# A hybrid encoder layer on one core: weight blocks of `up_sums` loaded half an item later, pools changed ahead of the output additions, `h2d` loaded by ScalarE in pairs

## The chip, the cores and the metric

The kernel runs on one core of a Trainium2 chip. The metric is the device time of one execution in microseconds; less is better. The kernel before takes 2178.68 us, the median of three runs (2177.78 to 2183.35).

Names used below: PE is TensorE (PEld its weight loads), DVE is VectorE, ACT is ScalarE, POOL is GpSimd, SP is SyncE, whose queue issues most of the DMAs in order. "L863" is line 863 of the kernel before.

## What is computed

The reference is one layer of a streaming encoder for a prompt of 2048 tokens and a sample of 64, model width 1024, with states carried for the sample:

```python
h = rmsnorm(x, g1) * (1 + sc1) + sh1
proj = h @ w_in                          # pool input u, q, k, v, o, gates
pool_out = pool_mixer(u, ...)            # causal means of 2, 4, 8, 16 tokens
hs = mlstm_seq(q, k, v, gates, ...)      # 4 heads, chunks, state C, n, m
mix = concat([pool_out, norm(hs) * sigmoid(o)], -1) @ w_out
x = x + gt1 * mix
h2 = rmsnorm(x, g2) * (1 + sc2) + sh2
up = h2 @ w_up                           # width 2 * 2816
conv = b_conv + sum(w_conv[j] * upp[:, j:j + T] for j in range(3))
a, g = split(conv, 2, -1)
x = x + gt2 * ((silu(g) * a) @ w_down)
```

A final rmsnorm follows, and the new states are returned. Everything is in float32.

## The kernel before, in words

Every matrix product is done in three passes of float32r: a tile is split into a high part (a copy, by ACT) and a low part (a subtraction, by DVE), and high x high, high x low and low x high are added up in PSUM. Weights come from HBM as a stream in the order of use: `issue` (L384) loads the next unit, `work_on` (L407) splits it (L411 on ACT, L414 on DVE), and `pump` (L421) keeps several units ahead, at most five of them still unsplit.

**Attention half.** The tokens go in four groups (`for o in groups`, L1432): 512 tokens each, the last one with the 64 of the sample besides. A group runs `proj_v` (the v columns and the gates), then four heads with three products each (q, k, o: 12 calls of `gemm`), then the four pooling blocks, then `outproj` (L617): eight output rows of 128, the first two as a pair, then six single ones. In the last group the pair ends with `leave` (L1419), which works off the generators that are left, stores the states, closes the pools of the attention half (`actx`) and opens pool `f1`, whose tiles `fscr` and `ssum` take that memory.

**FFN half.** It works on three groups of 704 tokens. The up-projection uses a scheme of Strassen's kind: a 2 x 2 block product is done with seven products instead of eight, on sums of blocks. Sums of weight blocks come from `up_sums` (L844), those of the activations from `sums_of` (L757). For the first group `norm_sums` (L795) reads the normed rows from `h2d` in HBM into four `fscr` tiles, in pairs for each of four blocks `kc`, and writes seven named tiles of sums, high and low, into `hx`. For each name ACT writes the high part (L782) and DVE the low part (L768); DVE also forms the next sums in place (L764). The first FFN products (L1573) read `hx`: the first of them, B11, needs that name of all four blocks.

**What sets the order.** Side work is written as generators in five lists (`bg`). `tick(i)` (L106) takes one step of the first generator of list i, and `gemm` (L467) calls ticks at fixed places among its eight column blocks. `up_sums` is in list 4: `gemm` steps it after the blocks in `ups`, by default (1, 3, 4, 6), unless `quiet` is set, as it is from the pooling blocks until the pair of output rows is nearly done. `proj_v` steps it four times a group. `norm_sums` is in list 1, stepped seven times in an output row once `f1` is open. The steps only write the program down: within the attention half a planner then orders each engine's instructions by priority, which follows the order of writing, and by readiness in its own model of time. `keep_in_program_order` (here also `pin`) holds an instruction behind the one written before it on its engine. In the FFN half PE, ACT, DVE and POOL keep the order of writing. Semaphores are placed by the compiler. An engine's queue is in order: what waits at its head holds up all behind it. That is also true of DMA issues on SP and ACT.

**`up_sums`.** It starts in group 1, has 44 items (22 blocks f in two halves) and a ring of four tiles `w4`. Three items are loaded ahead (two DMAs each, L849). An item takes four steps: two empty ones, two DVE instructions (L863, L864), two more (L866, L867); then the item three ahead is loaded (L871) and this one is stored to `wsum` (L872). That load takes the tile whose store was issued an item earlier and has to wait for it.

Of the kernel before, what the change touches and what calls it, by code (L numbers as in the profile page):

```python
# [25 lines left out]
FT = 704  # L26
# [38 lines left out]
def tile_layer(ctx: ExitStack, tc: tile.TileContext, xT, vecs, cst, rst, w_mod, w_ada, w_qkou, w_v, w_pool,  # L65
               w_out, w_up, w_down, w_quad, st_C, st_pool, yT, o_pool, o_C, o_m, o_conv):
    nc = tc.nc
# [399 lines left out]
    def gemm(ps, W, mv, o, ks=None, order=None, late=None, ups=(1, 3, 4, 6)):  # L467
        order = order or list(range(len(mv)))
        ks = ks or order
        for k in ks:  # L470
            if late is not None and k == late:
                drain(0, 2)
            at = order.index(k)
            U = W.at(at // 4)
            for pi, (a, b) in enumerate(PASSES):
                for bi, (lo, hi) in enumerate(o.blks):
                    pe.matmul(ps[bi][:, :hi - lo], U[:, a, k % 4 * P:(k % 4 + 1) * P], mv[k][:, b, lo:hi],  # L477
                              start=(at == 0 and pi == 0), stop=(k == order[-1] and pi == 2))
            if at in (1, 2, 4, 6, 7):
                tick(0)  # L480
            if at in ups and not quiet:
                tick(4)
            if at == 3 and o.last and not spare:
                tick(1)
            if at == 4 and not quiet and not spare:
                tick(3)
            if spare and at in (1, 2, 3, 4, 5, 6):
                tick(1)
        for i in (1, 3):
            tick(i)  # L490
        for gen in list(bg[2]):
            if next(gen, 0) == 0:
                bg[2].remove(gen)
# [98 lines left out]
    def load_x(k, o):  # L592
        x = scr()
        nc.sync.dma_start(out=x[:, :o.T], in_=xT[k, :, o.t0:o.t0 + o.T])
        return x
# [18 lines left out]
        rstd_cols([ssum], o, out)  # L614
        yield

    def outproj(o, mix, between):  # L617

        order = [4, 5, 6, 7, 3, 2, 1, 0]
        ssum = None if o.last else ssum_tile()  # L620
        now = Urgent(nc.vector)
        nx = [load_x(n, o) for n in (0, 1)]
        for rows in [(0, 1)] + [(n,) for n in range(2, KD)]:
            xs = nx
            Ws = [Row() for _ in rows]
            pss = [[mm_ps() for _ in o.blks] for _ in rows]
            if len(rows) == 1:
                gemm(pss[0], Ws[0], mix, o, order=order, ups=(4,))
            else:
                for W, ps in zip(Ws, pss):  # L630
                    gemm(ps, W, mix, o, ks=order[:6], order=order)
                quiet.clear()
                for W, ps in zip(Ws, pss):
                    gemm(ps, W, mix, o, ks=order[6:], order=order, late=1)
            nx = [load_x(rows[-1] + 1, o)] if rows[-1] + 1 < KD else []
            for n, x, ps in zip(rows, xs, pss):
                for (bi, pa, pb, a, b, s) in o.pieces:
                    now.scalar_tensor_tensor(out=x[:, a:b], in0=ps[bi][:, pa:pb], scalar=gt1(n, s), in1=x[:, a:b],
                                             op0=ALU.mult, op1=ALU.add)
                nc.sync.dma_start(out=x2d[n, :, o.t0:o.t0 + o.T], in_=x[:, :o.T])  # L640
            if rows[0] == 0:
                between()
                if o.last:
                    ssum = fscr("ssum")
            for n, x in zip(rows, xs):
                sq_acc(ssum, x[:, :o.T], o.T, n == 0)
        if o.last:
            bg[0].append(stat2(o, ssum))
        else:
            side.append(rstd_rows(ssum, o, RS2[:, 4 * o.g:4 * o.g + len(o.chunks)], []))  # L650
# [12 lines left out]
    def fscr(dt=F32):  # L663
        if dt in ("rb", "ssum"):
            return spare[0].tile([P, FT], F32, tag=dt, name=dt)
        return spare[0].tile([P, FT], dt, tag="fscr", name="fscr", bufs=4)
# [128 lines left out]
    def norm_sums(o, B, scr):  # L795

        xs = {}

        def load(kc):
            xs[kc] = [scr(), scr()]  # L800
            for x, k in zip(xs[kc], (kc, kc + 4)):
                (act if kc < 2 else nc.sync).dma_start(out=x[:, :FT], in_=h2d[k])
        load(0)
        yield
        for kc in range(4):
            if kc < 3:
                load(kc + 1)
            yield from sums_of(xs.pop(kc), lambda nm: (B.at(nm, kc, 0), B.at(nm, kc, 1), lambda: None))

    def prepare(o, scr):  # L810

# [25 lines left out]
    if True:  # L837
# [6 lines left out]
        def up_sums():  # L844

            def load(f, c):
                w = a1.tile([P, 4, 256], F32, tag="w4", name="w4", bufs=4)
                for i in range(2):
                    tc.keep_in_program_order(nc.sync.dma_start(out=w[:, 2 * i:2 * i + 2, :], in_=w_up[NF * i + f].rearrange(  # L849
                        "p (h c) -> p h c", h=2)[:, :, c:c + 256]))  # L850
                return w
            todo = [(f, c) for f in range(NF) for c in (0, 256)]
            pin = tc.keep_in_program_order
            nx = [load(*todo[i]) for i in range(3)]
            yield
            yield
            for i, (f, c) in enumerate(todo):
                w = nx.pop(0)
                yield
                yield  # L860

                a0, a1_, g0, g1 = (w[:, i, :] for i in range(4))
                pin(dve.tensor_tensor(out=g1, in0=g0, in1=g1, op=ALU.add))  # L863
                pin(dve.tensor_tensor(out=g0, in0=a0, in1=g0, op=ALU.subtract))  # L864
                yield
                pin(dve.tensor_tensor(out=a0, in0=g1, in1=a0, op=ALU.subtract))  # L866
                pin(dve.tensor_tensor(out=a1_, in0=a1_, in1=a0, op=ALU.subtract))  # L867
                yield

                if i + 3 < len(todo):  # L870
                    nx.append(load(*todo[i + 3]))  # L871
                pin(nc.sync.dma_start(out=wsum[f, :, :, c:c + 256], in_=w))  # L872

        def fold():
# [541 lines left out]
        def nothing():  # L1416
            pass

        def leave():  # L1419

            drain(1, 2, 3, 4)
            nc.sync.dma_start(out=o_pool, in_=PO)
            nc.sync.dma_start(out=o_C[:, 0], in_=SP[0])
            nc.sync.dma_start(out=o_C[:, 1], in_=SN)
            nc.sync.dma_start(out=o_m[0], in_=M[:, GT:GT + 1])
            nc.sync.dma_start(out=o_m[1], in_=M[:, TMAX + 1:TMAX + 2])
            actx.close()
            spare.append(fctx.enter_context(tc.tile_pool(name="f1", bufs=1)))
            B.append(Sums())
            bg[1].append(norm_sums(fgroups[0], B[0], fscr))  # L1430

        for o in groups:  # L1432
# [61 lines left out]
                bg[2].append(pg)  # L1494
            drain(1)
            if o.last:
                outproj(o, mix, leave)
            else:
                bg[1].append(norm_apply(groups[o.g + 1], box, hn))
                outproj(o, mix, nothing)  # L1500
# [792 lines left out]
```

## Time and profile before

| what | value |
|---|---|
| median of the runs | 2178.68 us |
| profiled execution, its own time | 2178.68 us |
| its span, first to last instruction | 2176.9 us |
| granted TensorE clock, mean | 0.998 |
| DMA moved | 539.51 MB, mean 248 GB/s |
| PE on the chain that ended last | 83% of the span |
| DVE / DMA / issue on that chain | 7% / 6% / 2% |
| attention half | 0 to about 793 us |
| FFN half | from about 793 us |

How to read it: the profile is of one execution. A view of groups gives busy time, the mean duration of one instruction, and the idle time of the engine just before, with what ended it ("<-"). A view of waits gives who waited for whom: total us, times, longest. A busy PE isn't PE at its peak, since matmuls are pipelined. The view of stages gives the busy time of each engine in a stretch. The `x` counts instructions. "SPq" and "ACTq" are the DMA issues and waits of those queues.

### The profile page before, as it was taken

The numbers are of one execution on the slowest core, as the hardware profiler recorded it, in microseconds if no ns is written. First come the engines' busy times: TensorE is split into PE (matmuls) and PEld (weight loads), VectorE is DVE, ScalarE is ACT, GpSimd is POOL, SyncE is SP. The second block draws the span as 40 slices with busy tenths as digits, with TensorE's granted clock in tenths as the row PEclk, the third lists the DMA queues.
The fourth block names the chain that finished last, engine by engine and source line by source line (L and its number), as shares of the span: only waits on it lengthen the run. The fifth ranks groups of instructions, "written<-read, shape, count | busy, mean of one in ns | idle before, by whom it ended". The sixth has DMA issues, their size and how long they took to land.

```text
span 2176.9 us, 38052 instructions
## 1 busy us (share of the span) xinstructions
PE 2151.8 (99%) x13553; PEld 2044.1 (94%) x13553; DVE 1634.7 (75%) x3040; ACT 1094.2 (50%) x2181; POOL 252.3 (12%) x475
## 2 busy tenths in 40 slices
PE   8999999999999999999999999999999999999998
PEld 7888888888899999999999999999999999999998
DVE  5868669767855678797967669888887597887874
ACT  4554335234333456464736446655655364565554
POOL 0010000001000101010101120100100321111112
PEclk9999999999999999999999999999999999999999
DMA  8887997998879477798967976666668675555542
GB/s 323 326 300 229 311 310 261 312 293 277 299 242 310 133 268 257 265 314 286 347 220 253 313 251 222 238 201 218 229 211 272 231 257 182 172 177 189 174 160 81
DMA packets 297351, 539.51 MB, mean 248 GB/s; under 512 B 25760, under 2 KB 114336, under 8 KB 297160
## 3 DMA queue, kind: packets, MB, share of 16 engines
q1 hardware_dynamic: 287144, 513.31, 70.7%
q10 hardware_dynamic: 10016, 23.76, 2.8%
q8 instruction: 107, 1.75, 0.3%
q14 instruction: 84, 0.69, 0.1%
HBM read 410.98 MB, written 125.98 MB: 247 GB/s over the span
## 4 chain that ended last, share of the span: by engine, by line
PE 83%; DVE 7%; DMA 6%; issue 2%; ACT 2%; SPq 0%; POOL 0%; ACTq 0%; DVEq 0%; POOLq 0%
PE mm L1573 33%; PE mm L477 21%; PE mm L2139 12%; PE mm L2016 8%; PE mm L1118 2%; DVE wt L414 2%; DMA wt<-wsum 1%; DMA raw<-w_ada 1%; PE m L1308 1%; PE m L1330 1%; PE m L1328 1%; PE m L1293 1%; DMA w<-w_ada 1%; DVE tg L1551 1%; DMA raw<-w_qkou 0%
## 5 line engine op out<-in xcount | busy, mean ns | idle before, releaser
L1573 PE MATMUL mm<-hx,wt 128*128 128x352 f32 x5544 | 886.7, 321 | 3.3 <-DVE hx L768 2.4
L1573 PEld LDWEIGHTS mm<-hx,wt 128*128 128x128 f32 x5544 | 878.3, 188 | 6.3 <-DVE hx L768 3.2
L477 PE MATMUL mm<-hl,wt 128*128 128x512 f32 (+2 forms) x1920 | 387.4, 357 | 0.1
L411 ACT ACTIVATE wt<-raw 128x512 fp32r<-128x512 f32 (+3 forms) x470 | 276.7, 597 | 185.1 <-PE mm L477 63.9
L414 DVE TENSOR_TENSOR wt<-raw,wt 128x512 fp32r<-128x512 f32 (+3 forms) x470 | 313.5, 673 | 65.4 <-ACT wt L411 65.2
L477 PEld LDWEIGHTS mm<-hl,wt 128*128 128x128 f32 x1920 | 316.7, 189 | 47.7 <-issue 4.4
L2139 PE MATMUL mm<-av,wt 128*128 128x448 f32 (+1 forms) x1632 | 262.8, 322 | 0.0
L2139 PEld LDWEIGHTS mm<-av,wt 128*128 128x128 f32 x1632 | 250.5, 188 | 11.1
L1988 DVE SCALAR_TENSOR_TENSOR x<-mm,MOD,x 128x352 f32<-128x352 f32 (+3 forms) x360 | 168.0, 508 | 78.7 <-PE mm L2139 65.1
L2016 PE MATMUL mm<-av,wt 128*128 128x352 f32 x1344 | 220.6, 323 | 1.7 <-DVE x L1988 0.7
L2016 PEld LDWEIGHTS mm<-av,wt 128*128 128x128 f32 x1344 | 215.4, 188 | 4.8 <-DVE ea L1582 2.7
L1620 ACT ACTIVATE mm<-mm 128x352 f32<-128x352 f32 x196 | 87.8, 448 | 237.7 <-PE mm L1573 181.5
L477 PE MATMUL mm<-mx,wt 128*128 128x512 f32 (+1 forms) x960 | 182.6, 352 | 0.0
L477 PEld LDWEIGHTS mm<-mx,wt 128*128 128x128 f32 x960 | 159.3, 188 | 22.5
L1551 DVE SCALAR_TENSOR_TENSOR ta<-ea,V,ta 128x704 f32<-128x704 f32 (+1 forms) x132 | 125.7, 953 | 58.6 <-ACT ta L1546 54.6
L1551 DVE SCALAR_TENSOR_TENSOR tg<-eg,V,tg 128x704 f32<-128x704 f32 (+1 forms) x132 | 125.7, 952 | 56.6 <-ACT tg L1546 54.1
L414 DVE TENSOR_TENSOR wt<-wt 128x512 fp32r<-128x512 f32 x196 | 133.4, 687 | 8.6 <-ACT wt L411 8.6
L411 ACT ACTIVATE wt<-wt 128x512 fp32r<-128x512 f32 x196 | 119.2, 622 | 29.5 <-DMA wt<-wsum 28.5
L1529 POOL COPY ea<-UC 128x2 f32<-128x2 f32 x66 | 32.5, 493 | 505.5 <-DVE ta L1551 410.9
L1760 ACT ACTIVATE tg<-tg 128x704 f32<-128x704 f32 (+1 forms) x66 | 52.4, 795 | 71.6 <-DVE tg L1551 71.6
L1118 PE MATMUL mm<-wt,hl 128*128 128x256 f32 (+1 forms) x576 | 71.4, 284 | 0.0
L1118 PEld LDWEIGHTS mm<-wt,hl 128*128 128x128 f32 x576 | 70.4, 190 | 0.8 <-issue 0.6
(305 smaller groups left out, 2202.1 us busy)
## 6 DMA issues: line engine op xcount, KB each, us to landing
wt<-wsplit SPq DMA_DIRECT2D x132, 512.0 KB, 4.3
raw<-w_up SPq DMA_DIRECT2D x198, 256.0 KB, 4.0
wt<-hl_kept SPq DMA_DIRECT2D x96, 512.0 KB, 6.1
wt<-wsum SPq DMA_DIRECT2D x132, 256.0 KB, 5.2
wsplit<-wt SPq DMA_DIRECT2D x66, 512.0 KB, 5.5
w<-w_up SPq DMA_DIRECT2D x88, 256.0 KB, 3.7
wsum<-w SPq DMA_DIRECT2D x44, 512.0 KB, 4.9
Bd<-fscr ACTq DMA_DIRECT2D x56, 352.0 KB, 4.1
```

Of the source, the lines that this page charges most:

```text
L411: act.activation(u.w[:, 0, :u.n], u.raw[:, :u.n], AF.Copy)
L414: dve.tensor_tensor(out=u.w[:, 1, :u.n], in0=u.raw[:, :u.n], in1=u.w[:, 0, :u.n].bitcast(F32), op=ALU.subtract)
L477: pe.matmul(ps[bi][:, :hi - lo], U[:, a, k % 4 * P:(k % 4 + 1) * P], mv[k][:, b, lo:hi], start=(at == 0 and pi == 0), stop=(k == order[-1] ...
L1118: pe.matmul(ps[ti][:n, :cols], h[4 * kh + k4][:, b, lo:lo + n], U[:, a, k4 % 2 * cols:(k4 % 2 + 1) * cols], start=(kh == 0 and k4 == 0 and ...
L1529: pool.tensor_copy(ext[:, 0:2], UC[:, f, :])
L1551: dve.scalar_tensor_tensor(out=t[:, :E], in0=ext[:, j:j + E], scalar=wc(j, f), in1=t[:, :E], op0=ALU.mult, op1=ALU.add)
L1573: pe.matmul(bk.t[:, :FH], U[:, a, kc * P:(kc + 1) * P], Bo.at(nm, kc, b), start=(first and kc == 0 and pi == 0), stop=(kc == 3 and pi == 2 ...
L1620: act.activation(to.t[:, :FH], bk.t[:, :FH], AF.Copy)
L1760: act.activation(self.tg[:, :E], self.tg[:, :E], AF.Silu)
L1988: dve.scalar_tensor_tensor(out=x3[n][:, a:b], in0=bk.t[:, a - lo:b - lo], scalar=gt2(n, s), in1=x3[n][:, a:b], op0=ALU.mult, op1=ALU.add)
L2016: pe.matmul(bk.t[:, :FH], U[:, a, c:c + P], quad.put(op, m, b), start=(first and m == 0 and pi == 0), stop=(m == 1 and pi == 2), skip_grou ...
L2139: pe.matmul(bks[i].t[:, :hi - lo], U[:, a, k % 4 * P:(k % 4 + 1) * P], av[k][:, b, lo:hi], start=(k == 0 and (a, b) == PASSES[0]), stop=(k ...
```

## The change

It has four parts.

1. `outproj` steps `up_sums` after blocks 2 and 5 of a single row, where it was after block 4 alone.
2. In `outproj` `between` (in the last group: `leave`) is called ahead of the additions to the output rows, where it was behind them. The stores of the states are taken out of `leave` into `states`, which is called behind the first of the pair's two last gemm parts, when the heads are done.
3. `norm_sums` issues all loads of `h2d` on ACT. Two blocks are loaded at the first step, the third and fourth behind the second name of the block before. Before, one block was loaded ahead and the next one at the beginning of each block, the last two on SP.
4. `up_sums` loads an item in the first of the two empty steps, two items ahead, behind the store of the item before. The number of loaded items at the start is the same.

```diff
-    def outproj(o, mix, between):
+    def outproj(o, mix, between, behind_heads=None):
...
-                gemm(pss[0], Ws[0], mix, o, order=order, ups=(4,))
+                gemm(pss[0], Ws[0], mix, o, order=order, ups=(2, 5))
...
                 for W, ps in zip(Ws, pss):
                     gemm(ps, W, mix, o, ks=order[6:], order=order, late=1)
+                    if behind_heads:
+                        behind_heads()
+                        behind_heads = None
             nx = [load_x(rows[-1] + 1, o)] if rows[-1] + 1 < KD else []
+            if rows[0] == 0:
+                between()
             for n, x, ps in zip(rows, xs, pss):
...
-            if rows[0] == 0:
-                between()
-                if o.last:
-                    ssum = fscr("ssum")
+            if rows[0] == 0 and o.last:
+                ssum = fscr("ssum")
...
-                (act if kc < 2 else nc.sync).dma_start(out=x[:, :FT], in_=h2d[k])
-        load(0)
+                act.dma_start(out=x[:, :FT], in_=h2d[k])
+        for kc in (0, 1):
+            load(kc)
         yield
         for kc in range(4):
-            if kc < 3:
-                load(kc + 1)
-            yield from sums_of(xs.pop(kc), lambda nm: (B.at(nm, kc, 0), B.at(nm, kc, 1), lambda: None))
+            for i, _ in enumerate(sums_of(xs.pop(kc), lambda nm: (B.at(nm, kc, 0), B.at(nm, kc, 1), lambda: None))):
+                yield
+                if i == 1 and 0 < kc < 3:
+                    load(kc + 1)
...
                 w = nx.pop(0)
                 yield
+                if i and i + 2 < len(todo):
+                    nx.append(load(*todo[i + 2]))
                 yield
...
-                if i + 3 < len(todo):
-                    nx.append(load(*todo[i + 3]))
                 pin(nc.sync.dma_start(out=wsum[f, :, :, c:c + 256], in_=w))
...
-        def leave():
-
-            drain(1, 2, 3, 4)
+        def states():
+
             nc.sync.dma_start(out=o_pool, in_=PO)
             nc.sync.dma_start(out=o_C[:, 0], in_=SP[0])
             nc.sync.dma_start(out=o_C[:, 1], in_=SN)
             nc.sync.dma_start(out=o_m[0], in_=M[:, GT:GT + 1])
             nc.sync.dma_start(out=o_m[1], in_=M[:, TMAX + 1:TMAX + 2])
+
+        def leave():
+
+            drain(1, 2, 3, 4)
             actx.close()
...
-                outproj(o, mix, leave)
+                outproj(o, mix, leave, states)
```

## The prediction

> **What bounds the kernel now.** I read the engines' busy times first, then who TensorE (PE) waited for, then the stages.
>
> ```profile
> span 2176.9 us, 38052 instructions
> PE 2151.8 (99%) x13553; PEld 2044.1 (94%) x13553; DVE 1634.7 (75%) x3040; ACT 1094.2 (50%) x2181; POOL 252.3 (12%) x475
> ```
>
> ```profile
> PE m L1283 <- DVE GL L250: 3.2, 1, 3.2
> PE m L1308 <- DVE kw L250: 2.5, 2, 1.7
> PE mm L1573 <- DVE hx L768: 2.4, 3, 1.3
> PE mm L1573 <- ACT hx L782: 0.6, 2, 0.3
> ```
>
> PE is idle for 2176.9 - 2151.8 = 25.1 us in all, so that is the most that any change of waits can bring. No matmul is removed here. Of the waits inside the kernel two are within its reach: 3.2 us at L1283 (head loop of the last group) and 2.4 + 0.6 = 3.0 us at the first FFN products (L1573), which wait for the sums `hx`. By stages (columns: us, then busy time of PE, PEld, DVE, ACT, POOL, clock, DMA share, GB/s):
>
> ```profile
> 350.00:602.00 252.00, 252.00 (x1428) 217.74 (x1427) 198.10 (x399) 99.85 (x219) 12.42 (x18) 1.00 0.89 294
> 602.00:632.00 30.00, 26.77 (x195) 26.39 (x194) 16.94 (x42) 8.68 (x27) 1.11 (x1) 0.95 0.73 239
> 632.00:741.00 109.00, 109.00 (x808) 103.19 (x807) 66.69 (x177) 44.89 (x141) 14.19 (x21) 1.00 0.72 230
> 741.00:757.00 16.00, 16.00 (x122) 16.00 (x121) 8.54 (x18) 5.08 (x10) 1.07 (x4) 1.00 0.45 136
> 757.00:769.00 12.00, 12.00 (x92) 12.00 (x91) 4.11 (x9) 1.95 (x3) 0.36 (x2) 1.00 0.98 332
> 769.00:793.00 24.00, 24.00 (x182) 24.00 (x181) 21.99 (x50) 15.94 (x33) 0.00 (x0) 1.00 0.70 230
> 793.00:811.00 18.00, 15.02 (x91) 13.65 (x90) 13.70 (x28) 8.85 (x19) 0.00 (x0) 1.00 0.83 280
> 811.00:870.00 59.00, 59.00 (x372) 58.70 (x372) 46.79 (x69) 40.86 (x71) 10.94 (x21) 1.00 0.79 262
> ```
>
> The rows show where: 602 to 632 lacks 3.23 us of PE, 793 to 811 lacks 2.98, and the stretches between them are full. DVE is nearly full from 769 to 793 (21.99 of 24), just before PE stalls, and two thirds empty in the 12 us before that. So the sums for the first products begin too late, not too slowly. Why they begin at 769:
>
> ```profile
> 757.06 1.59 SPq L872 DMA_DIRECT2D wsum<-w  x2
> ```
>
> ```profile
> 762.91 0.69 ACT L508 ACTIVATE ssum<-scr 128x576 f32<-128x576 f32 x1 [0.92 <-DVE wt L414]
> 762.93 1.90 ACTq L802 DMA_DIRECT2D fscr<-h2d  x4
> 769.04 0.50 ACT L782 ACTIVATE hx<-fscr 128x352 fp32r<-128x352 f32 x1 [5.45 <-DMA fscr<-h2d]
> ```
>
> The last two stores of `up_sums` go out from 757.06. Their tiles (`w4`) are in a pool that must be closed before `fscr` and `ssum` get its memory. At the 4 to 5 us that such a store takes (row below), the second one lands near 763, which is when ScalarE (ACT) starts `ssum` and the loads of `h2d`. Those land at 769, in a stretch whose DMA share is 0.98.
>
> **The change, part by part.** *1. More steps of `up_sums` in the output projection.* Its 44 items take 2 + 4 x 44 = 178 steps and a last one. A group has 4 steps in `proj_v`, 4 in each of 12 gemms of the heads, 2 in the first pair of output rows and 1 in each of six further rows: 60. In groups 1 to 3 that gives 60 + 60 + 4 + 48 + 2 = 174 steps by `leave`, so the last item is worked off by the drain there: that is the pair of stores at 757. With 2 steps a row a group has 66, and step 179 falls on 179 - 132 = the 47th of group 3, inside its last head: before the output projection begins, 5/4 + 4 gemms of 51.27 / 8 = 6.4 us are still to come (the `mx` row below), 34 us. The work that moves: three items, about 1.5 into each of the output projections of groups 1 and 2, both inside 350 to 602.
>
> ```profile
> L863 DVE TENSOR_TENSOR w<-w x44: 404/420/428, 228.4 to 755.8; 128x256 f32<-128x256 f32 x44
> ```
>
> ```profile
> w<-w_up SPq DMA_DIRECT2D x88, 256.0 KB, 3.7
> wsum<-w SPq DMA_DIRECT2D x44, 512.0 KB, 4.9
> ```
>
> An item is four DVE instructions of 0.42 us (1.7 us; the other three have the same form), two loads of 256 KB and a store of 512 KB, 1.05 MB. Three items are 5 us of DVE and 3.1 MB. DVE has 252 - 198 = 54 us free there; DMA has 0.11 x 252 = 28 us free, and 3.1 MB at 294 / 0.89 = 330 GB/s takes 9.5 us. I cost this at 0, hidden under PE's 252.00 of 252.00; if the output projection had no cover, it would cost up to 9.5 us.
>
> *2. Pools changed ahead of the additions, outputs stored behind the heads.* What else holds the old memory until when:
>
> ```profile
> 741.81 51.27 PEld L477 LDWEIGHTS mm<-mx,wt 128*128 128x128 f32 x384
> 743.15 0.34 SPq L1422 DMA_DIRECT2D o_pool<-PO  x1
> 744.29 0.81 DVE L250 SCALAR_TENSOR_TENSOR scr<-s,u 128x512 f32<-128x512 f32 x2
> ```
>
> ```profile
> DMA to landing us min/median/max: 4.0/6.1/8.0
> ```
>
> PE is done with the old `hl` when it turns to `mx` at 741.8, the pooling with `u` and `s` at 745.1, and the store of `o_pool` starts at 743.15. So without the `w4` stores the `h2d` loads can go at about 748, between two of ACT's weight splits, 15 us earlier. The second row is how long they take (line 802); with a DMA share of 0.45 in this stretch I take 5, so the sums begin near 753 and not at 769. The bound on one side is 0 (something else still holds the memory), on the other 769.04 - 745.1 - 4.0 = 20 us. How much of it counts:
>
> ```profile
> L768 DVE TENSOR_TENSOR hx<-fscr,hx 128x352 fp32r<-128x352 f32 x28 | 13.5, 526 | 6.6 <-ACT hx L782 6.6
> L764 DVE TENSOR_TENSOR fscr<-fscr 128x352 f32<-128x352 f32 x16 | 8.2, 525 | 0.0
> ```
>
> That is 44 DVE instructions of about 0.53 us, 23 us. From 753 to 769 DVE has 4/16 x 7.46 + 7.89 = 9.8 us free, and 1.7 more since the last item is gone. So the sums could end about 11 us earlier; PE needs 3 to 4. Even a bubble of 3 us at each of the two later load pairs leaves it enough. Term: -3.0 us.
>
> The five output stores move ahead by half a row pair; one of them already stands in SP's queue before its data is there:
>
> ```profile
> SPq L1423 <- DVE SP L250: 8.1, 1, 8.1
> ```
>
> SP loses 8.1 us, and PE loses none of it in 632 to 741 (109.00 of 109.00), since the code loads up to five raw weight units ahead. I cost the move at 0; without that lead, 8.1 us.
>
> *3. `h2d` by ACT in pairs.* Now the loads for the third and fourth block stand in SP's queue and wait there for DVE:
>
> ```profile
> L802 SPq EVENT_SEMAPHORE  x5: 17/17/5212, 772.0 to 786.2; - x5
> ```
>
> The longest wait is 5.2 us. On ACT, behind the second name of the block before, the same wait would hold up ACT's own conversions. But at that place ACT's next conversion needs DVE to have got past the same point, so I cost it at 0, with 5.2 us either way as bounds (SP freed of it, or ACT held by it). Four more DMA issues of 0.5 us on ACT lie in 769 to 793, where ACT has 8 us free.
>
> *4. Load behind the store in `up_sums`.* The stall at L1283, first on SP, then in the chain of waits, then on DVE:
>
> ```profile
> 611.31 0.56 SPq L872 DMA_DIRECT2D wsum<-w  x1
> 616.10 1.20 SPq L849 DMA_DIRECT2D w<-w_up  x2
> 617.36 0.60 SPq L872 DMA_DIRECT2D wsum<-w  x1
> 621.73 1.20 SPq L849 DMA_DIRECT2D w<-w_up  x2
> ```
>
> ```profile
> 611.31 4.77 DMA wsum<-w
> 617.36 4.31 DMA wsum<-w
> 622.32 5.22 DMA w<-w_up
> ```
>
> ```profile
> 617.80 0.41 DVE L863 TENSOR_TENSOR w<-w 128x256 f32<-128x256 f32 x1
> ...
> 627.56 0.43 DVE L863 TENSOR_TENSOR w<-w 128x256 f32<-128x256 f32 x1 [7.66 <-DMA w<-w_up]
> 629.28 0.17 DVE L250 COPY GL<-m 128x20 f32<-128x20 f32 x1
> ```
>
> A load needs the buffer whose store was issued four items earlier in the rotation, and the next store is queued behind that load. So store, load, store, load land one after the other (4.77, 4.31, 5.22), DVE stands 7.66 us at the head of its queue, and the copy of `GL` stands behind it; PE goes on when that copy ends at 629.5, so by the 3.2 us of its wait it asked at 626.3. With the load a step later and behind the store, the store of 617.36, whose data was there (DVE's row of 617.80 is already the next item), would go some 5 us earlier, right behind that of 611.31, the load of 621.73 near 617, and DVE would go on at 622 to 623. `GL` would then be ready near 625, before 626.3. Term: -3.2 us. Bounds: -3.2, and +1.6 where the load, one step (a quarter of a 6.4 us gemm) later, is itself what is late.
>
> **Sum.** -3.0 - 3.2 = -6.2 us, from the profiled execution: span 2176.9 and 1.8 around it, 2178.7, which is also the median of the runs. Forecast 2178.7 - 6.2 = **2172.5**.
>
> PE's idle may be too small a measure of a stall, since ends of matmuls are modelled. The weight loads (PEld) are missing 30 - 26.39 = 3.6 us in the first stall and 18 - 13.65 = 4.35 in the second, against 0.3 in the 59 us after it. By these rows the gain is 7.9 us. The Trainium skill ("Perfetto Trace Analysis", Identifying the Most-Contended Engine) says that matmul busy time misjudges headroom and that weight-load busy time is to be taken; the trace shows both numbers and cannot tell yet which one the span follows.
>
> **Rivals.**
> - *Both stalls go, and count as PEld has them:* 2178.7 - 7.9 = 2170.8. For it: five short stops in a row, each with a restart. Against: some stop will be left.
> - *Only the transition is mended:* 2175.7. The order on DVE around 627 is a planner's, which puts an item's first instruction ahead of `GL`; it may do so again, with another load late.
> - *The start isn't moved, or not usefully* (something else in the old pools holds `fscr` until 760 or so): 2178.7 - 3.2 = 2175.5, or 2178.7 if the other stall stays too.
> - *Given back in the heads:* a new order of 3,040 DVE instructions brings one or two stops like the 3.2 us one elsewhere between 213 and 741: 2178.7 - 6.2 + 2 x 3.2 = 2178.9, up to 2182.
> - *Slower, by ACT:* the second halves of the `h2d` loads wait at the head of ACT's queue. Two waits of 5.2 us are 10.4 us of held conversions, for `hx` and for the first FFN weights. It decides once the start gains less than about 10.4 - 8 = 2.4 us; with no gain there PE stalls 10.4 us longer: 2189. For it: the 5.2 us stood on SP. Against: the 11 us of head start.
>
> **How the numbers follow.** Forecast 0.30; PEld's measure 0.15; transition alone 0.25; start not moved 0.10; given back 0.10; slower by ACT 0.10. 0.3% (6.5 us) is about what a measurement of this kernel can tell from no change; it lies at 2172.1 and 2185.2. Faster by more: 0.15 and a quarter of the forecast's case, 0.22. Slower by more: 0.10. Within: 0.68. The range reaches from just under PEld's measure, 2170, to 2182, the top of what is given back; it leaves out the 2189 and a little at each end.
>
> **What would show it.** Right: no store of `wsum` after about 730; the first `h2d` load on ACT before 752 and the first L782 before 758; no PE wait for `hx`; DVE idle between 790 and 800 again; no DVE wait of over 3 us at L863 between 600 and 640. Wrong: ACT idle before L782 or L411 behind L802; PE idle inside 350 to 602 (DMA share there over 0.97); a new PE wait in the heads.

## The result, and the profile after

The changed kernel takes 2181.43 us, the median of 22 runs (2178.84 to 2185.75), against 2178.27 for the kernel before in 22 runs beside it (2174.94 to 2183.35). The ratio is 1.0016, with a 95% interval of 1.0009 to 1.0022: slower by 2.0 to 4.8 us, where 2172.5, 5.8 us less than those runs, had been forecast. (In this part "L1581" and the like are lines of the changed kernel; L854, L877 and L870 are the load, the store and the first DVE instruction of an `up_sums` item, before L849, L872 and L863.)

The head of the page of the profile after (own time 2183.01 us, span 2181.2):

```profile
span 2181.2 us, 38069 instructions
PE 2155.0 (99%) x13553; PEld 2048.7 (94%) x13553; DVE 1632.8 (75%) x3040; ACT 1093.2 (50%) x2181; POOL 252.0 (12%) x475
```

PE and DVE have as many instructions to do as before. PE's idle time is 2181.2 - 2155.0 = 26.2 us, against 25.1. Whom PE waited for, after (us in total, times, longest):

```profile
PE m L1313 <- DVE kw L250: 6.9, 3, 3.6
PE mm L1123 <- DVE scr L250: 1.5, 1, 1.5
PE mm L477 <- ACT va L250: 1.0, 1, 1.0
```

Both waits that the forecast was built on, for `GL` and for `hx`, are gone from this list. Others have come: `kw` rose from 2.5 to 6.9, and two are new. By stages, after:

```profile
350.00:602.00 252.00, 246.87 (x1367) 211.73 (x1366) 193.18 (x398) 96.66 (x214) 11.82 (x18) 0.99 0.86 290
602.00:632.00 30.00, 29.05 (x225) 28.68 (x224) 20.91 (x46) 10.35 (x26) 1.34 (x1) 1.00 0.89 304
...
757.00:769.00 12.00, 12.00 (x93) 12.00 (x92) 11.72 (x27) 7.71 (x16) 0.00 (x0) 1.00 0.66 212
769.00:793.00 24.00, 24.00 (x183) 24.00 (x182) 23.22 (x53) 13.33 (x28) 0.00 (x0) 1.00 0.76 260
793.00:811.00 18.00, 18.00 (x120) 18.00 (x118) 5.94 (x11) 5.78 (x11) 0.00 (x0) 1.00 0.69 216
```

The stretch that was to be full cover, 350 to 602, has lost 5.13 us of PE and 0.01 of the clock. From 757 to 769 DVE is full where it was two thirds idle, with the DMA share down from 0.98 to 0.66: the sums run there now. The last stretch is full, and DVE is two thirds idle there: the sums were ready early.

Where the time goes is seen best from the start of the same matmul in two traces. Both programs issue 13,553 matmuls in one order, so the n-th start of one less the n-th start of the other is the delay at that point. The table gives what the delay grows by between two marks (times of the kernel before; worked out from all matmul rows; us). "Second" and "third" are further profiles of the same kernel.

```
kernel (profile)           0-350  350-390 390-420 420-450 450-590 590-615 615-650 650-780 780-870 870-2100
before, second              +2.2    0.0     0.0     0.0     0.0     0.0    -0.8     0.0    -1.0    -0.1
changed                     +0.1    0.0    +1.8    +5.4     0.0    +1.4    -4.7     0.0    -3.8    +4.1
changed, second             +4.6    0.0    +1.7    +5.9     0.0    +1.3    -3.7     0.0    -3.8    +2.6
changed, third              +0.5    0.0    +4.1    +3.9     0.0    +0.9    -4.0     0.0    -3.8    -0.7
e1 steps only               +1.4    0.0    +1.0    +4.4    +0.3    +0.1    -1.2    +1.3    -3.8    -0.3
e2 load only                +0.7    0.0     0.0    +4.9     0.0     0.0    -4.4    +0.2    +1.9    +2.2
e2 load only, second        +4.1    0.0     0.0    +3.2     0.0     0.0    -4.7     0.0    -1.3    -0.7
e3 pools and h2d            +1.7    0.0     0.0     0.0     0.0    +0.3    -0.3     0.0    -3.8    -0.7
e5 changed, one step        +1.6    0.0     0.0    +6.4     0.0     0.0    -4.7    +1.8    -3.8    +0.3
e6 changed, old load        -0.6    0.0    +1.4    +3.8     0.0    +0.6    +0.9     0.0    -3.8    +0.7
e9 late load                +0.3    0.0     0.0     0.0     0.0    +0.7    -4.6     0.0    -3.8    -0.3
e9 late load, second        -1.1    0.0     0.0     0.0     0.0     0.0    -4.6    +1.6    -3.8    +0.7
```

A stop of PE makes a positive number, a stall that is mended a negative one. The first and the last column differ between executions of one kernel by up to 4.8 us. In the columns between, a kernel's stops come again at the same places, but not in the same size: two profiles of one kernel differ there by up to 3.2 us (e2, 780 to 870), and the 1.6 us of e9 between 650 and 780 came in one profile of two. The stalls that the change was to mend vary too: in e11, whose edit lies behind the stall at 626, that stall cost 2.6 us less than in the first profile of the kernel before.

**The two gains came.** On ACT, after, around the transition:

```profile
749.49 0.35 ACTq L805 DMA_DIRECT2D fscr<-h2d  x1
...
749.87 1.53 ACTq L805 DMA_DIRECT2D fscr<-h2d  x3
...
754.66 1.26 ACT L785 ACTIVATE hx<-fscr 128x352 fp32r<-128x352 f32 x3
```

The last store of `wsum` goes out at 705.2 (758.1 before), the loads of `h2d` 13 us earlier, and the first sums 14 us earlier.

**A loss of 7 us lies in front of them**, in the output projection and the first head of the third group. On DVE, after, where PE's longest wait comes from:

```profile
431.11 0.16 DVE L543 TENSOR_SCALAR RS<-m 128x4 f32<-128x4 f32 x1
439.79 0.75 DVE L210 SCALAR_TENSOR_TENSOR s<-raw,CA,s 128x512 f32<-128x512 f32 x1 [8.52 <-DMA raw<-w_ada]
...
441.78 0.17 DVE L250 COPY GL<-m 128x16 f32<-128x16 f32 x1
...
443.19 0.68 DVE L250 TENSOR_TENSOR kw<-m,CL 128x512 f32<-128x512 f32 x1
```

L210 is `ada`, another background job: in each of the last three groups it multiplies 16 blocks of `w_ada` by the conditioning vector and adds them up. DVE stands 8.52 us at the head of its queue for one of these blocks, and `GL` and `kw`, which PE needs, stand behind it. It is the form of the stall that was to be mended at 626, with another load. Before, the same instruction waited a little too, and PE lost nothing by it:

```profile
433.71 0.75 DVE L210 SCALAR_TENSOR_TENSOR s<-raw,CA,s 128x512 f32<-128x512 f32 x1 [1.99 <-DMA raw<-w_ada]
```

Why that block is late is seen in SP's queue. Before:

```profile
412.66 2.28 SPq L194 DMA_DIRECT2D raw<-w_ada  x3
...
418.42 0.55 SPq L194 DMA_DIRECT2D raw<-w_ada  x1
...
421.16 0.55 SPq L194 DMA_DIRECT2D raw<-w_ada  x1
...
427.57 0.56 SPq L872 DMA_DIRECT2D wsum<-w  x1
...
428.86 0.96 SPq L194 DMA_DIRECT2D raw<-w_ada  x1
431.10 1.20 SPq L849 DMA_DIRECT2D w<-w_up  x2
```

After:

```profile
416.94 2.29 SPq L854 DMA_DIRECT2D w<-w_up  x2
...
419.93 0.62 SPq L877 DMA_DIRECT2D wsum<-w  x1
...
421.27 1.53 SPq L194 DMA_DIRECT2D raw<-w_ada  x1
...
428.76 0.56 SPq L877 DMA_DIRECT2D wsum<-w  x1
429.37 3.04 SPq L854 DMA_DIRECT2D w<-w_up  x4
...
433.41 0.81 SPq L194 DMA_DIRECT2D raw<-w_ada  x2
...
436.19 1.32 SPq L194 DMA_DIRECT2D raw<-w_ada  x2
```

And whom SP waited for between 421 and 437, after:

```profile
SPq L877 <- DVE w L874: 5.0, 1, 5.0
```

Before, no load or store of `up_sums` was issued between 407 and 427.5, and the five `w_ada` loads of the rows from 412.66 to 421.16 went out ahead of that store; one was left behind it. After, SP stands 5.0 us at a store whose data DVE has not finished, then issues four loads of `w_up`, and only then the next `w_ada`, which goes out at 433.4 and is used at 439.8; four of these loads are behind the store. The stop at 393 (the column 390 to 420) has the same form: `ada` waits 5.95 us on DVE, and the addition behind it holds up PE at L1123.

```profile
392.40 0.49 DVE L208 TENSOR_SCALAR u<-raw,CA 128x512 f32<-128x512 f32 x1 [5.95 <-DMA raw<-w_ada]
392.80 0.75 DVE L250 SCALAR_TENSOR_TENSOR scr<-mm,MOD,scr 128x512 f32<-128x512 f32 x1
```

### The profile page after: what moved, and what is told of

The parts are those of the page before. It is cut to its first block, busy times and chain, and to the rows that moved or that the text cites. A ratio compares the mean times of both kernels' runs of the same rounds, so it can differ in the third digit from the quotient of the medians.

```text
span 2181.2 us, 38069 instructions
## 1 busy us (share of the span) xinstructions
PE 2155.0 (99%) x13553; PEld 2048.7 (94%) x13553; DVE 1632.8 (75%) x3040; ACT 1093.2 (50%) x2181; POOL 252.0 (12%) x475
## 4 chain that ended last, share of the span: by engine, by line
PE 83%; DVE 7%; DMA 6%; issue 2%; ACT 1%; SPq 1%; POOL 0%; DVEq 0%; POOLq 0%; ACTq 0%
PE mm L1581 36%; PE mm L477 20%; PE mm L2147 11%; PE mm L2024 8%; DMA raw<-w_ada 2%; DVE wt L414 1%; PE mm L1123 1%; PE m L1313 1%; PE m L1335 1%; PE m L1333 1%; DVE scr L250 1%; PE mm L1059 1%; PE m L1298 1%; DVE s L210 1%; DMA raw<-w_up 1%
## 5 line engine op out<-in xcount | busy, mean ns | idle before, releaser
L1581 PE MATMUL mm<-hx,wt 128*128 128x352 f32 x5544 | 889.7, 322 | 1.3 <-DVE wt L414 0.7
L1581 PEld LDWEIGHTS mm<-hx,wt 128*128 128x128 f32 x5544 | 882.8, 188 | 2.8 <-DVE wt L414 1.3
L1123 PE MATMUL mm<-wt,hl 128*128 128x256 f32 (+1 forms) x576 | 71.6, 284 | 1.5 <-DVE scr L250 1.5
L1123 PEld LDWEIGHTS mm<-wt,hl 128*128 128x128 f32 x576 | 70.4, 190 | 2.6 <-DVE scr L250 1.7
```

The costliest lines, as they stand in the source:

```text
L1123: pe.matmul(ps[ti][:n, :cols], h[4 * kh + k4][:, b, lo:lo + n], U[:, a, k4 % 2 * cols:(k4 % 2 + 1) * cols], start=(kh == 0 and k4 == 0 and ...
L1581: pe.matmul(bk.t[:, :FH], U[:, a, kc * P:(kc + 1) * P], Bo.at(nm, kc, b), start=(first and kc == 0 and pi == 0), stop=(kc == 3 and pi == 2 ...
```

## The experiments

The theory: the loss is made by loads of `w_ada` that stand in SP's queue behind `up_sums`, brought there by the extra steps (part 1), by the moved load (part 4), or by both. The rivals: another part does harm; or the loss is not in the heads but in the FFN's products, by chance of the execution. Ratios are to the kernel before, run beside each kernel (medians of 2177.4 to 2178.0), with their 95% intervals.

**e1: the steps alone**, on the kernel before:

```diff
-                gemm(pss[0], Ws[0], mix, o, order=order, ups=(4,))
+                gemm(pss[0], Ws[0], mix, o, order=order, ups=(2, 5))
```

> Only the two steps per output row (ups=(2, 5)) on the kernel before. Theory A (the new stops around 393 and 432 to 440 come from the shifted phase of up_sums against the head loop, which this edit causes): a PE stop of 4 to 8 us between 390 and 450 as in the changed kernel, the transition stall at 793 to 811 gone or smaller (the last store of wsum goes out before 730), 2178 to 2183 us. Theory B (they come from the load's later place in up_sums): no new stop between 390 and 450, the transition mended by about 3.5 us, 2173 to 2176. Theory C (the loss is only the slower cadence of the FFN's products, by chance of the run): 2172 to 2176 in some executions, above 2178 in others.

Measured: 2181.79 us, 1.0018 (1.0009 to 1.0027). Theory A's stop is there (+1.0 and +4.4 in the table; DVE's wait for `w_ada` before it is 6.42 us), and the transition is mended (-3.8): the last store of `wsum` goes out at 708.5.

**e2: the load alone**, on the kernel before:

```diff
                 yield
+                if i and i + 2 < len(todo):
+                    nx.append(load(*todo[i + 2]))
                 yield
...
-                if i + 3 < len(todo):
-                    nx.append(load(*todo[i + 3]))
                 pin(nc.sync.dma_start(out=wsum[f, :, :, c:c + 256], in_=w))
```

> Only the load moved behind the store in up_sums, on the kernel before. Theory A (phase of the extra steps is to blame): no PE stop of over 2 us between 390 and 450, the stall at 626 to 629.5 gone, the transition stall still there: 2174 to 2176. Theory B (the load's place is to blame): a PE stop of 4 to 8 us between 390 and 450 and the queue of SP with loads of w_up ahead of the one of w_ada: 2178 to 2184. The waits of SP for its own stores (99 us before) fall to about 20 us under both.

Measured: 2183.21 us, 1.0021 (1.0012 to 1.0030). So A and B do not exclude each other: either part alone brings the stop at 437 (here +4.9, and +3.2 in the second profile). In both, loads or stores of `up_sums` now stand in the gap that they had left in SP's queue before. SP, with only the load moved:

```profile
419.49 1.21 SPq L849 DMA_DIRECT2D w<-w_up  x2
...
421.45 0.56 SPq L872 DMA_DIRECT2D wsum<-w  x1
422.06 0.62 SPq L194 DMA_DIRECT2D raw<-w_ada  x1
...
428.32 1.25 SPq L849 DMA_DIRECT2D w<-w_up  x2
...
430.94 0.59 SPq L194 DMA_DIRECT2D raw<-w_ada  x1
```

The stall at 626 is gone here, and the transition's is not. SP's waits for its own stores fell from 99.2 to 28.0 us. The columns from 350 to 870 add up to +2.6 and -2.8 us in the two profiles, while the runs are slower by 2.6 to 6.5: part of what this edit costs isn't placed by them.

**e3: pools, states and `h2d` alone**, on the kernel before: parts 2 and 3 of the diff of the change, that is all of it but the line with `ups` and the lines of `up_sums`.

> Only the pools changed ahead of the additions, the state outputs earlier and h2d by ScalarE in pairs, on the kernel before. With the last two wsum stores still at 757, theory (all parts of the gain at the transition hang on the extra steps): h2d loads still go out near 762, PE stop at 793 to 811 still 2 to 4 us, 2177 to 2180. Rival (moving the pool change alone starts the sums earlier): stop gone, 2174 to 2176. Second rival (ScalarE held at the head of its queue by the second pair): the stop grows by 5 us or more, 2183 to 2189.

Measured: 2175.43 us, 0.9988 (0.9979 to 0.9997). The rival had it right: without one extra step the transition is mended in full.

```profile
793.00:811.00 18.00, 18.00 (x116) 17.97 (x116) 7.57 (x16) 6.37 (x13) 1.56 (x2) 1.00 0.69 223
```

With `leave` called ahead of the additions its drain is written ahead of them too; the last item of `up_sums` is done earlier, and its store goes out at 746.6 in place of 758.1:

```profile
L877 SPq DMA_DIRECT2D wsum<-w x44: 554/562/1310, 247.6 to 746.6; - x44
```

**e4: the changed kernel once more**, with no edit.

> The changed kernel once more, unaltered. Theory C (slow cadence of the FFN's products by chance): in this profile the three stretches of 166.7 ns a product (908 to 970 and two shorter ones) are elsewhere or missing, and the span differs by 3 to 4 us. If it belongs to the kernel: the same stretches again, span 2180 to 2182. The stops at 393 and 432 to 440 are there in either case.

Measured: 2181.93 us, 1.0023 (1.0013 to 1.0033); profiled span 2185.3. The stops at 393 and 437 are the same. Of the three stretches of slow products (in which the FFN's products run at the slower of two paces, see the last section) two are there again and the third is not.

**e5 and e6: the changed kernel without the steps, and without the moved load.** The diffs of e1 and e2 undone, one at a time.

> The changed kernel with one step per output row again (the load moved, pools and h2d as changed). From the parts measured alone: stop near 437 about +5 us (the load's place), stall at 626 gone (-4.4), transition mended by the pool change without the extra steps (-3.8), slow products between 909 and 972 (+2.4) if they belong to the moved load: 2176 to 2180. Rival (the transition needs the early end of up_sums): stop for hx back at 793, 2181 to 2184.

> The changed kernel with the load of up_sums at its old place (two steps, pools and h2d as changed). Parts alone: stop near 437 about +5, stall at 626 a little smaller (-1), transition -3.8 once, since both parts mend the same stall; no slow products between 909 and 972 if those belong to the moved load: 2178 to 2182. Rival (the slow products are chance): they show here too, 2180 to 2184.

Measured: 2179.24 us, 1.0005 (0.9993 to 1.0017), and 2181.68 us, 1.0022 (1.0011 to 1.0032). Every effect is there with its part: before 615 e5 has the stop at 437 (+6.4) and no other; e6 has 393 and 437 (+1.4, +3.8) and keeps the stall at 626. The stop at 393 comes with the steps (e1, e6) and not with the load (e2, e5). What both parts bring, the stop at 437, counts once and not twice in the changed kernel, and so does the transition, which parts 1 and 2 both mend. The column 590 to 615 is +0.9 or more only in the changed kernel as it is, and was not taken apart further.

**e7: the loads of `w_ada` issued by ACT**, in the changed kernel:

```diff
                 got[i] = raw_tile()[:, :512]
-                nc.sync.dma_start(out=got[i], in_=src[i])
+                act.dma_start(out=got[i], in_=src[i])
```

> The changed kernel with the w_ada loads of the later groups issued by ScalarE and not by SP. Theory (the stop at 437 comes from w_ada loads that stand in SP's queue behind a store of wsum that waits 5.0 us for DVE, and behind four loads of w_up): the loads go out before 430, DVE's wait of 8.5 us at 431 shrinks below 3, no PE stop of over 2 us at 437, 2174 to 2177. Rival (the DMA engines, not the queue, make them late; or the ada work itself is late on DVE): the wait stays over 5 us, 2180 to 2184. Second rival: the loads now hold up ScalarE while they wait for a raw buffer, new stops for ACT's products, 2182 or more.

Measured: 2184.47 us, 1.0030 (1.0019 to 1.0042). The theory holds for the stop at 437, the second rival for the time. The loads that had gone out at 433.4 to 436.9 now go out at 414.9 to 419.4:

```profile
412.69 1.17 ACTq L194 DMA_DIRECT2D raw<-w_ada  x2
413.91 0.38 ACT L250 ACTIVATE va<-mm 128x256 f32<-128x256 f32 x1 [3.90 <-DMA raw<-w_ada]
414.93 0.33 ACTq L194 DMA_DIRECT2D raw<-w_ada  x1
...
419.36 0.33 ACTq L194 DMA_DIRECT2D raw<-w_ada  x1
```

The stop at 437 is gone (0.0 in the column 420 to 450), and DVE waits for none of these loads between 420 and 440: it was the order in SP's queue that made them late. But these loads now stand among ACT's conversions; `va` at 413.91 comes behind two of them. The column 390 to 420 is +7.7, of which 4.6 is a wait of PE that ends there (the longest of the two below) and the rest the slower clock behind it (last section). In the waits of PE, over the whole span:

```profile
PE mm L1123 <- ACT va L250: 7.2, 2, 4.6
```

The Trainium skill ("Trainium Kernel Development and Optimization", Key Constraints) says that issuing DMAs from several engines only saves the sequencer's issue time; here it changed the time of issue by 17 to 19 us, because what a queue holds up at its head differs from one engine to the other.

**e8: the stores of `wsum` issued by GpSimd**, in the changed kernel:

```diff
-                pin(nc.sync.dma_start(out=wsum[f, :, :, c:c + 256], in_=w))
+                pin(pool.dma_start(out=wsum[f, :, :, c:c + 256], in_=w))
```

> The changed kernel with the stores of wsum issued by GpSimd. Theory (what makes the loads late is SP standing at a store whose data DVE has not finished): SP has no wait of over 2 us between 421 and 432, w_ada loads out by 428, the PE stop at 437 under 2 us, 2174 to 2178. Rival (the loads of w_up ahead of w_ada are enough to make it late): stop still 4 us or more, 2179 to 2183.

Measured: 2215.57 us, 1.0176 (1.0160 to 1.0192). This says nothing on its question: the stores now stand in POOL's order, POOL stands for tens of us ahead of some of them, and PE loses 4.1 to 13.5 us in each of the five columns from 390 to 650.

```profile
423.38 0.71 POOL L877 DMA_DIRECT2D wsum<-w  x1 [32.70 <-DVE s L208]
```

**e9: the load moved for the late items only** (`i` counts the items from 0), with parts 2 and 3 and without part 1:

```diff
+                if i > 28 and i + 2 < len(todo):
+                    nx.append(load(*todo[i + 2]))
                 yield
...
-                if i + 3 < len(todo):
+                if i < 28:
                     nx.append(load(*todo[i + 3]))
```

> Pools and h2d as changed, one step per row, and the load of up_sums moved only for the items from the 29th on, which run in the last group's projections and heads (before them the old place). Theory (the load's place costs about 5 us at 437, where items 16 to 20 run, and gains about 4 us at 626, where items 34 and 35 run): no PE stop of over 2.5 us at 437, none at 626, no PE wait for hx: 3.5 to 4 us below the kernel with only the pools changed, 2170.5 to 2173. Rival (a load moved anywhere shifts the planner's order and brings another stop in the last heads): 2174 to 2179.

Measured: 2172.89 us, 0.9976 (0.9967 to 0.9985), faster than both kernels. The three stretches in question, in this trace, which runs 4 us ahead at the last of them:

```profile
420.00:450.00 30.00, 30.00 (x155) 25.44 (x154) 21.60 (x49) 10.59 (x30) 2.01 (x2) 1.00 0.92 308
602.00:632.00 30.00, 29.76 (x224) 29.05 (x222) 18.92 (x47) 9.73 (x30) 1.89 (x1) 1.00 0.90 301
785.00:803.00 18.00, 18.00 (x119) 18.00 (x117) 8.73 (x18) 7.62 (x15) 0.00 (x0) 1.00 0.71 219
```

Both gains are kept, and the only new stop in this profile is of 0.7 us, between 590 and 615. How the stall at 626 is mended, on DVE:

```profile
621.09 0.43 DVE L870 TENSOR_TENSOR w<-w 128x256 f32<-128x256 f32 x1 [7.48 <-DMA w<-w_up]
...
625.04 0.17 DVE L250 COPY GL<-m 128x20 f32<-128x20 f32 x1
```

DVE still stands 7.48 us for a load, but the wait ends at 621 and no longer at 627.6, so `GL` is copied before PE asks for it. In the changed kernel it is the same with 6.84 us.

**e10 and e11: part 2 alone and part 3 alone**, on the kernel before. The core of the one and of the other:

```diff
+            if rows[0] == 0:
+                between()
             for n, x, ps in zip(rows, xs, pss):
```

```diff
-                (act if kc < 2 else nc.sync).dma_start(out=x[:, :FT], in_=h2d[k])
+                act.dma_start(out=x[:, :FT], in_=h2d[k])
```

> Only the pools changed ahead of the output additions and the states stored earlier, h2d as before. Theory (draining up_sums ahead of the additions is what frees the memory early: last wsum store 746 in place of 758): h2d loads near 752, no PE wait for hx over 0.5, 2174 to 2176.5. Rival (the pairs by ScalarE are needed, since the later loads in SP's queue come late): a stop of 1.5 to 3 us at 793 to 811 stays, 2176.5 to 2178.5.

> Only h2d loaded by ScalarE in pairs on the kernel before. Theory (the start at 763 is what is late): loads still from 762, stop at 793 to 811 within 1 us of the 3 us before, 2177 to 2179. Rival (the waits of the later loads on SP made the stop): stop under 1 us, 2174 to 2176. Second rival (ScalarE held by the second pair, up to 10.4 us): 2180 to 2189.

Measured: 2175.69 us, 0.9990 (0.9981 to 0.9999), and 2178.18 us, 0.9999 (0.9990 to 1.0008). Part 2 mends the transition by itself (-3.8 there), with loads of `h2d` from 750.6; part 3 does nothing that can be told from zero, and its loads go out from 760.8.

**e12: `w_ada` loaded five steps ahead**, in the changed kernel:

```diff
-        lead = 4 if first else 3
+        lead = 4 if first else 5
```

> The changed kernel with the w_ada loads of the later groups issued five steps ahead and not three. Theory (the loads stand too late in SP's queue, behind the store that waits for DVE): the last loads of group 2's share go out before 425, the stop at 437 falls below 2 us, 2175 to 2178. Rival (the five raw buffers, shared with the weight stream, hold them back or now hold back the weights): the stop stays or new PE waits for wt, 2181 to 2188.

Measured: 2183.58 us, 1.0021 (1.0012 to 1.0031). The time and the stop that stays are the rival's. The last three loads go out at 436.4 to 439.5, against 433.8 to 436.9 at the lead of three; but this kernel is 8.8 us behind the kernel before at that point and the changed one 1.8, so by the same matmul they go out some 4 us earlier. DVE's longest wait there is 3.9 us in place of 8.5, and the column 420 to 450 falls from +5.4 to +3.8. In exchange the column 390 to 420 rises to +5.1, where DVE waits 7.7 us for an earlier one of these loads. SP still stands 4.0 us at a store of `wsum` ahead of them. What the five raw buffers do in this was not taken apart.

**e13 to e16: second and third profiles**, with no new edit, for the slow stretches of products.

> The kernel before, a second profile. If the slow stretches of FFN products (166.7 ns apart in place of 158.3) follow the kernel: none of over 60 products, as in its first profile. If they are chance of the execution: one or more stretches, at any place.

> The kernel with only the load moved, a second profile. If the slow stretches follow the kernel: 379 products at 166.7 ns from about 912 to 975 again, 2.4 us. If chance: missing or elsewhere.

> The changed kernel, a third profile. If the slow stretches follow the kernel: 71 products near 797 and 379 from about 909 again. If chance: one of them missing or elsewhere. The stops near 393 and 437 are there in either case, those at 626 and for hx are not.

> The kernel of the late load, a second profile. If the slow stretches follow the kernel: 71 products near 790 and 81 from 948, none of 379. If chance: elsewhere. No PE stop of over 2.5 us at 437, none at 626, in either case; 2170 to 2175.

Measured: 2179.05, 2179.82, 2179.70 and 2171.81 us. The stretch of 379 products is in two of three profiles of the changed kernel and in one of two with the load alone, each time from the same product on, and in none of the nine profiles of kernels whose early items have the load at its old place. The profiles of e5, e7, e8 and e12, with the moved load, lack it too. So whether it comes in an execution is chance; whether the moved load makes it likelier, and so is to be charged with it, these few profiles do not settle. The one of 71 products at the beginning of the FFN is in every profile in which the transition is mended in full (62 products in e8), and in neither of the kernel before.

## Why the prediction was wrong, point by point

- **Part 1, cost 0 (the step that failed).** It was "hidden under PE's 252.00 of 252.00", with 54 us of DVE and 28 us of DMA free. The cover was there as a sum and not at the place: over the stretch neither DVE nor DMA was short of time (DMA share 0.86 after), but the queues of SP and DVE hand a wait on in order: a load of `w_ada` stood behind a store on SP, DVE stood for that load, and PE for DVE. The steps cost 5.3 us there (e1, columns 390 to 450). Of the prediction's signs of being wrong, "PE idle inside 350 to 602" and "a new PE wait in the heads" came; a DMA share over 0.97 there did not.
- **Part 4, term -3.2.** The mechanism at 626 was borne out: in e9 the store went out at 612.23, the load at 615.75, DVE went on at 621.09, and `GL` "near 625" was 625.04. The sign "no DVE wait of over 3 us at L863" was not right (7.48 us): what counts is when the wait ends. The size was 3.7 to 4.7 us against the first profile of the kernel before, and less against an execution in which the stall was shorter; the last section says why. (The load moves by one of an item's four steps, a quarter of an item, where the title has half.) What was left out is that the edit moves the loads of nearly all 44 items and not of the one at 626. At items 16 to 20 it puts loads and stores ahead of `w_ada`, for 3.2 to 6.4 us (e2, e5). The bound of +1.6 for a load that is "itself what is late" looked at the `up_sums` loads only, not at what stands behind them on SP.
- **Transition, term -3.0.** It came, at -3.8. The prediction has it under part 2 but lets it rest on the early end of `up_sums` by part 1. Either part does it alone (e1, e10), so the steps, which brought the stops, were not needed for it.
- **Part 3, cost 0, and the rival by ACT.** Right: 0.9999 in e11, and no wait of 5.2 us came on ACT.
- **PEld's measure.** 4.35 us of weight loads were missing in the transition and 3.6 at 626; the delays say 3.8 and up to 4.7. PE's idle, 3.0 and 3.2, was too small in both places, and PEld isn't exact either. The Trainium skill ("Perfetto Trace Analysis", Identifying the Most-Contended Engine) says that matmul busy time misjudges headroom; the transition agrees (3.0 of idle, 3.8 gained). At 626 the difference is the clock's (last section), which the prediction's bound of 25.1 us by PE's idle time left out too.
- **The rival that happened is "given back in the heads"**, which had a chance of 0.10 and "one or two stops like the 3.2 us one" for a price. The stops at three places (columns 390 to 420, 420 to 450 and 590 to 615) came to 8.6, 8.8 and 8.9 us in the three profiles, against 8.5, 7.5 and 7.8 gained.

The sum, changed kernel (mean of three profiles) less kernel before (mean of two): the stops +2.5, +5.0 and +1.2, the stall at 626 -3.8, the transition -3.3, together +1.7 before rounding; the start of the kernel +0.6 and the FFN +2.1, which vary by the execution; in all 4.4, where the runs show 2.0 to 4.8. So the stops undo the gains, and 1.7 us of the loss has a place; the rest is not shown to belong to the change. How much of the 2.1, in which the stretch of 379 products counts, would stay over many profiles isn't settled.

## What to carry to other kernels

Here a background job cost its place in the queues, not its busy time: before it is stepped more often or its loads are moved, look at which loads of other jobs go through in the gaps that it leaves on the issuing queue, and who stands behind those jobs on the computing engine. An edit in a loop is priced for every turn of the loop, not for the stall it was made for; where only some turns gain (here from `i` = 29 on), change only those. A fully busy engine over a long stretch is no cover for a wait of 5 us at one place in it.

## What the runs showed of the hardware

**A stop of PE of some 3 us can cost its length and then about 1.7 us of clock.** The changed kernel around the stop at 437 (clock in the third column from the end):

```profile
440.00:442.00 2.00, 0.43 (x2) 0.00 (x0) 2.00 (x5) 0.00 (x0) 0.00 (x0) 1.00 1.06 409
442.00:444.00 2.00, 0.00 (x0) 0.01 (x1) 2.00 (x5) 0.00 (x0) 0.00 (x0) 1.00 0.36 137
444.00:446.00 2.00, 1.98 (x11) 1.81 (x12) 2.00 (x4) 0.00 (x0) 0.00 (x0) 0.73 0.77 242
446.00:448.00 2.00, 2.00 (x6) 1.57 (x5) 1.58 (x4) 0.00 (x0) 0.00 (x0) 0.50 0.99 286
448.00:450.00 2.00, 2.00 (x12) 1.74 (x11) 0.37 (x2) 0.00 (x0) 0.00 (x0) 0.92 0.85 238
```

The clock is at half after PE has begun again: 2 x (0.27 + 0.50 + 0.08) = 1.7 us, on top of the wait of 3.6, which makes 5.3 of the 5.4 in the table. The stall at 626 in the kernel before has the same tail (0.73, 0.50, 0.91 from 628 to 634; the middle one below), which is why its removal was worth 4.7 and not 3.2; the 0.95 stood in the row of 602 to 632 that the prediction quoted, and was not counted.

```profile
630.00:632.00 2.00, 2.00 (x10) 2.00 (x10) 1.93 (x7) 0.00 (x0) 0.00 (x0) 0.50 0.29 109
```

In the clock records of all the traces every such drop ahead of the last 20 us of the kernel lasts 3.41 us at half clock, or twice or three times that (e7 and e8). Drops near 79 and 263 come in some executions and not in others (neither in the first profile of the kernel before, both in the second one of the changed kernel): up to 1.7 us each of what the first column varies by.

The length alone doesn't decide: between two starts of matmuls there were 2.4 us in e6 and 2.6 in the third profile of the changed kernel at 398, with the drop, and 3.4 us in the second profile of e2, without it. In e11 the stall at 626 is 2.2 us and has no drop. The Trainium skill ("TensorE: Matmul & The Clock Gate", Part 1) has half the clock after one idle window of about 3.4 us, in windows that run freely; the half clock agrees, a drop after 2.4 us does not, and 3.4 us without one fits windows that aren't tied to the stop.

**The FFN's products run at one of two paces.** 352 columns take 158.3 or 166.7 ns from start to start, at a clock of 1.00 with no wait shown, and keep the pace for 71 to 379 products. The group of these products from 912 to 965, first in the kernel before and then in the changed one:

```profile
L1573 PE MATMUL mm<-hx,wt 128*128 128x352 f32 x336 | 53.6, 321 | 0.0
```

```profile
L1581 PE MATMUL mm<-hx,wt 128*128 128x352 f32 x320 | 53.5, 328 | 0.0
```

It is 16 products fewer in 53 us, with PE busy throughout. The long stretch begins right behind a short pause: the two gaps between starts ahead of it take 0.45 to 0.87 us together, in place of 0.32. The stretch of 71 products, and some others, begin without one. What sets the pace was not found.
